# First stage of a two-layer attention and SSD kernel: order of the loads, tile-by-tile modulation, TensorE's order written out

## The chip, the cores and the metric

The kernel runs on one core of a Trainium2 chip. The metric is the device time of one execution in microseconds, the median of several runs. Inside a core, TensorE multiplies matrices, VectorE (DVE) and ScalarE (ACT) work on tensors elementwise, GpSimd (POOL) takes elementwise work as well, and SyncE's queue (SP) issues the loads and stores.

## What is computed

Two layers of a diffusion backbone run over 128 context tokens and 512 latent tokens, so five tiles of 128 tokens (tile 0 is the context), with width 1024. The change lies in the entry of layer 0: the normed input is scaled and shifted by a modulation that is itself a product of the condition with a weight, and is then projected to q, k, v and a gate.

```python
def rms_norm(x, w):
    y = xf * lax.rsqrt(jnp.mean(xf * xf, axis=-1, keepdims=True) + EPS)
    return y * w

def ada_mod(cond, mod_w, mod_b):
    m = jax.nn.silu(cond) @ mod_w + mod_b
    return jnp.split(m, 3, axis=-1)          # shift, scale, gate

def modulate(x, norm_w, shift, scale):
    return rms_norm(x, norm_w) * (1.0 + scale) + shift

def attn_qkvg(h, w_in, q_norm, k_norm):
    proj = h @ w_in
    q, k, v, g = jnp.split(proj, [...], axis=-1)
    ...
```

Behind it come attention with 16 heads over 4 key and value heads, the gated output projection, and layer 1 (a Mamba-2 mixer), which the change leaves alone.

## The kernel before

All products of activations and weights are made as three products of split operands: a value is cast to a high part (ScalarE, line 73), and the rest is a subtraction (VectorE or GpSimd, line 74); the pieces multiplied are high by high, high by low and low by high. The result keeps float32 accuracy.

The program is written as one stream of instructions. A planner with a timing model orders each engine's instructions and each queue's loads by itself, in the order of the text where nothing else speaks; each engine then executes its own list in that order and waits where an operand or a buffer isn't ready.

Layer 0 begins in `layer0` (line 285). The loads are issued in this order: the five tiles of x (line 328, 512 KB each; the small vectors `v0` of line 330 go in after the second), then four times a quarter: `load_mod(q)` (line 309) with four tiles of the modulation weight (512 KB each) and `load_kv(q)` (line 317) with 256 of the 1024 rows of the k, v weight (512 KB) and their split, whose subtractions run on GpSimd. A raw weight tile has two buffers.

Then the work, with the names of the program:

- `turned(t)` (line 339) takes a tile of x: sum of squares on ScalarE, reciprocal root on GpSimd (`norm_x`, line 226), scaling on VectorE, eight transposes on TensorE into `acc` and `pt`, and two copies back, one by ScalarE and one by VectorE.
- `mod(q)` (line 347) makes a quarter of shift and scale: 16 products into `pm` (each shows as two matmul instructions), a copy into `modrow` on ScalarE, four small products that turn the row into columns (line 357), and three small VectorE operations.
- `modded(q)` (line 366) applies them to two of the eight 128-row slices: for each slice once on tile 0 (128 columns) and once on tiles 1 to 4 together (512 columns), a scaling on VectorE into `hm`, the high part on ScalarE and the low part on VectorE, into `big`.
- `mm_kv(i, t, q)` (line 374) is the k (i = 0) or v (i = 1) product of a tile for a quarter: six matmuls into `acc`. There are 240 in all.

The text has all five `turned`, the columns of `v0`, then `mod(0)`, `modded(0)`, and for each quarter the next quarter's `mod` and `modded` ahead of the sixty matmuls of this one; in the third quarter the small vectors of layer 1 are prepared (`vectors`, line 152). At the end a ScalarE copy takes each tile's k and v to `kv` (line 396). Then `load_w` (line 255) loads and splits the first q weights, with subtractions on VectorE. `attention` (line 404) follows: it loads the first gate weights, norms and rotates k and q and starts the scores (line 630). Its q projection (line 283) writes into `S`, which takes the room of `acc`.

## Time and profile before

| | us |
|---|---|
| median of three runs | 1020.06 |
| lowest, highest | 1019.86, 1020.76 |
| span of the profiled execution, first to last instruction | 1016.4 |
| TensorE busy | 939.4 (92% of the span) |
| VectorE, ScalarE, GpSimd busy | 727.0, 549.4, 503.2 |
| mean granted TensorE clock | 0.978 |

The profiler gives the span of the execution that it recorded; that execution's time as the runs measure it is not listed. A timeline row has the start, the duration, the engine, the line of the program, the operation, what is written and read, and, in brackets, how long the engine had been idle before and what released it. Several equal instructions in a row are merged into one row (x4). PE is TensorE, SPq the issuing of SyncE's queue. [...]

### The profile page before, as it was taken

To read this page: it belongs to the slowest core of one execution; us is meant where nothing else is said; L and a number is where in the kernel's file an instruction comes from. 1 tells how busy PE (TensorE), PEld (TensorE's weight loads), DVE (VectorE), ACT (ScalarE), POOL (GpSimd) and SP (SyncE) were. 2 spreads that over 40 slices of the span, in tenths; PEclk is the share of its full clock that TensorE was granted. 3 is DMA by queue.
4 is the path that set the end of the run, shared out by engine and by line. 5 is a ranking of instruction groups with operands and counts; after the bars stand their busy time and mean duration, and the time that the engine had idled before them with its cause. 6 is when DMAs were issued, how large, how long until landed. Compare 5 with 4: busy or idle time off the path is not lost. (4 is left out here: it accounts for less than half of the span.)

```text
span 1016.4 us, 17297 instructions
## 1 busy us (share of the span) xinstructions
PE 939.4 (92%) x6522; PEld 847.7 (83%) x6522; DVE 727.0 (72%) x1094; ACT 549.4 (54%) x1272; POOL 503.2 (50%) x451
## 2 busy tenths in 40 slices
PE   5998999999999899989998898898988999889998
PEld 3898878989997789978997797788987999667786
DVE  5478665766776766757688788977688767996663
ACT  5346766757766653323465575567445664654340
POOL 3355325225450433445177679869487867642000
PEclk9999999999999999999999899998999999899999
DMA  9933242211122322333342345235324532446752
GB/s 312 350 120 104 92 142 89 84 52 43 42 64 84 104 87 102 125 100 96 99 137 91 104 147 171 68 129 160 111 90 133 178 110 89 135 147 193 256 194 100
DMA packets 90354, 127.91 MB, mean 126 GB/s; under 512 B 6816, under 2 KB 65312, under 8 KB 90272
## 3 DMA queue, kind: packets, MB, share of 16 engines
q1 hardware_dynamic: 90272, 126.82, 39.0%
q8 instruction: 51, 0.84, 0.3%
q14 instruction: 31, 0.25, 0.1%
HBM read 115.10 MB, written 11.70 MB: 125 GB/s over the span
## 5 line engine op out<-in xcount | busy, mean ns | idle before, releaser
L914 PE MATMUL pj<-h,wh 128*128 128x322 f32 (+1 forms) x1248 | 293.5, 320 | 6.2 <-DVE B L999 4.2
L74 POOL TENSOR_TENSOR wl<-raw,wh 128x512 fp32r<-128x512 f32 (+1 forms) x70 | 135.6, 1949 | 183.5 <-ACT wh L73 183.3
L914 PEld LDWEIGHTS pj<-h,wh 128*128 128x128 f32 (+1 forms) x1248 | 214.9, 192 | 11.0 <-issue 4.4
L914 PE MATMUL pj<-h,wl 128*128 128x322 f32 (+1 forms) x624 | 198.0, 318 | 0.0
L73 ACT CAST wh<-raw 128x1024 fp32r<-128x1024 f32 (+1 forms) x117 | 103.3, 912 | 81.8 <-DMA raw<-in_l_w_out 26.0
L914 PEld LDWEIGHTS pj<-h,wl 128*128 128x128 f32 (+1 forms) x624 | 120.2, 193 | 1.2 <-issue 0.2
L1140 ACT ACTIVATE am<-am,nb 128x128 f32<-128x128 f32 x320 | 98.6, 392 | 28.4 <-POOL am L1135 14.2
L283 PE MATMUL pp<-wh,big 128*128 128x256 f32 x576 | 113.4, 287 | 0.5 <-ACT sg L527 0.5
L283 PEld LDWEIGHTS pp<-wh,big 128*128 128x128 f32 x576 | 92.4, 191 | 0.7 <-ACT sg L527 0.7
L74 DVE TENSOR_TENSOR wl<-raw,wh 128x1024 fp32r<-128x1024 f32 x47 | 68.9, 1470 | 26.7 <-ACT wh L73 26.6
L283 PE MATMUL pp<-wl,big 128*128 128x256 f32 x288 | 81.8, 284 | 0.0
L74 DVE TENSOR_TENSOR pl<-pt,ph 128x512 fp32r<-128x512 f32 (+1 forms) x100 | 59.2, 600 | 25.9 <-ACT ph L73 25.0
L633 DVE TENSOR_REDUCE nm<-S 128x1 f32<-128x640 f32 x64 | 52.4, 820 | 13.6 <-PE S L630 12.7
L73 ACT CAST ph<-pt 128x512 fp32r<-128x512 f32 (+1 forms) x100 | 51.3, 518 | 18.8 <-PE pt L658 14.1
L637 ACT ACTIVATE Pt<-S,nm 128x640 f32<-128x640 f32 x64 | 51.3, 803 | 12.1 <-PE pt L658 9.5
L1141 POOL TENSOR_TENSOR am<-am,am 128x1024 f32<-128x1024 f32 x20 | 50.2, 2512 | 14.6 <-ACT am L1140 14.0
L1208 POOL TENSOR_TENSOR ys<-ys,ym 128x512 f32<-128x512 f32 x32 | 48.8, 1533 | 13.6 <-DVE ym L1207 13.6
L283 PEld LDWEIGHTS pp<-wl,big 128*128 128x128 f32 x288 | 55.0, 191 | 0.0
L658 PE MATMUL pt<-cst,Pt 128*128 128x128 f32 x320 | 50.8, 276 | 2.7 <-DVE pl L74 2.3
L630 PE MATMUL S<-kT,qT 128*128 128x320 f32 x256 | 50.6, 322 | 1.4 <-ACT Pt L637 1.4
L841 PE MATMUL a<-wh,big 128*128 128x256 f32 x256 | 46.8, 283 | 0.0
L658 PEld LDWEIGHTS pt<-cst,Pt 128*128 128x128 f32 x320 | 36.6, 141 | 11.9 <-PE S L630 3.8
(375 smaller groups left out, 2319.8 us busy)
## 6 DMA issues: line engine op xcount, KB each, us to landing
raw<-in_l_w_in SPq DMA_DIRECT2D x48, 512.0 KB
am<-acd SPq DMA_DIRECT2D x40, 512.0 KB
raw<-in_l_w_out SPq DMA_DIRECT2D x36, 512.0 KB
og<-in_l_mod_w SPq DMA_DIRECT2D x29, 512.0 KB
raw<-in_l_w_in SPq DMA_DIRECT2D x25, 256.0 KB
mw<-in_l_mod_w SPq DMA_DIRECT2D x11, 512.0 KB
raw<-in_l_mod_w SPq DMA_DIRECT2D x8, 512.0 KB
yzd<-ys SPq DMA_DIRECT2D x6, 640.0 KB
```

Source lines behind the costliest of these rows:

```text
L73: (heng.tensor_copy if heng else self.nc.scalar.copy)(hi, src)
L74: (eng or self.nc.vector).tensor_tensor(lo, src, r32(hi), op=ALU.subtract)
L283: nc.tensor.matmul(ps, a[:, k, cs], b[:, k, :], start=k == 0 and a is hi and b is w[0], stop=k == KD - 1 and a is lo)
L630: nc.tensor.matmul(S[:, 192 + 320 * q:512 + 320 * q], qTs[g, t][:, h, :], kT[:, hl, 320 * q:320 * q + 320], start=hl == 0, stop=hl == 1)
L633: nc.vector.tensor_reduce(c["m"], c["s"], axis=AX.X, op=ALU.max, negate=True)
L637: nc.scalar.activation(Pt, c["s"], AF.Exp, bias=c["m"], scale=1.0, accum_out=rss[g][t][:, h:h + 1])
L658: nc.tensor.transpose(pt[:, 2 * i + j, :], Pts[j][:, kt * P:kt * P + P], self.ident)
L841: self.nc.tensor.matmul(ps, self.ohl[a][:, k, ts], w[b][:, k, :], start=k == 0 and i == 0, stop=k == KD - 1 and i == 2)
L914: nc.tensor.matmul(ps[0:m, 190 + 322 * half:512 + 322 * half], w[b][:, k, off:off + m], hT[s][:, k, 322 * half:322 * half + 322], start=fi ...
L1140: nc.scalar.activation(af[d][:, h, :], af[d][:, h, :], AF.Exp, bias=self.nb[:, t, i:i + 1], scale=1.0)
L1141: nc.gpsimd.tensor_tensor(af[0], af[0], af[1], op=ALU.add)
L1208: nc.gpsimd.tensor_tensor(y, y, m, op=ALU.add)
```

## The change

The loads are issued in another order: the small vectors first, then tile 0 of x, the first quarter's modulation and k, v weights, then tiles 1 to 4 of x, then the other quarters. The split of a quarter's k, v weights is taken out of `load_kv` into `split_kv`, which stands behind the copy of that quarter's modulation row on ScalarE. `modded` takes a list of parts, so that the first quarter is modulated one tile at a time, with the next tile's `turned` ahead of this tile's matmuls. The second quarter's `mod` and `modded` follow after the first quarter's matmuls, and the third's and fourth's stand after two tiles of the quarter before. TensorE's instructions keep the written order from the columns to the last k, v matmul (`manual_schedule`). The vectors of layer 1 and the split of the first q weights are queued behind the last VectorE and ScalarE instructions of the stage (`issue_after`, an order on the engine's own list).

```diff
+    def last_on(self, engine):
+        return next(i for i in reversed(self.nc.cur_bb.bb.instructions) if i.engine == engine)
...
             def load_kv(q):
                 ks = slice(2 * q, 2 * q + 2)
-                raw = self.tl(self.wp, [P, 2, 512], tag="raw")
+                raw = raws[q] = self.tl(self.wp, [P, 2, 512], tag="raw")
                 nc.sync.dma_start(out=raw, in_=src[:, ks, D:D + 512])
-                for i, w in enumerate(wkv):
-                    self.split(w[0][:, ks, :], w[1][:, ks, :], raw[:, :, 256 * i:256 * i + 256], self.weng[0])
+
+            def split_kv(q):
+                ks = slice(2 * q, 2 * q + 2)
+                with tc.issue_after(self.last_on(mybir.EngineType.Activation)):
+                    for i, w in enumerate(wkv):
+                        self.split(w[0][:, ks, :], w[1][:, ks, :], raws[q][:, :, 256 * i:256 * i + 256], nc.gpsimd)
...
-            for t in range(NT):
-                nc.sync.dma_start(out=xs[:, t, :], in_=self.x_in(t))
-                if t == 1:
-                    v0 = self.column_rows(rp, "v0", 0, (("l0_norm_w", 8), ("l0_mod_b", 24)))
+            v0 = self.column_rows(rp, "v0", 0, (("l0_norm_w", 8), ("l0_mod_b", 24)))
             self.weng = [nc.gpsimd]
             for q in range(4):
+                if q == 0:
+                    nc.sync.dma_start(out=xs[:, 0, :], in_=self.x_in(0))
                 load_mod(q)
                 load_kv(q)
+                if q == 0:
+                    for t in range(1, NT):
+                        nc.sync.dma_start(out=xs[:, t, :], in_=self.x_in(t))
...
                 nc.scalar.copy(row, pm)
+                split_kv(q)
...
-            def modded(q):
+            def modded(q, parts=((0, 0, 1), (1, 1, NT - 1))):
                 for k in (2 * q, 2 * q + 1):
-                    for c, at, n in ((0, 0, 1), (1, 1, NT - 1)):
+                    for c, at, n in parts:
...
-            for t in range(NT):
-                turned(t)
-            self.columns(v0, 0, self.tl(pp, [P, 192], tag="pt"))
-            mod(0)
-            modded(0)
-            for q in range(4):
-                if q == 2:
-                    self.vectors(*vec, pp)
-                if q < 3:
-                    mod(q + 1)
-                    modded(q + 1)
+            with tc.manual_schedule(engines={mybir.EngineType.PE}):
+                self.columns(v0, 0, self.tl(pp, [P, 192], tag="pt"))
+                turned(0)
+                mod(0)
                 for t in range(NT):
+                    modded(0, ((min(t, 1), t, 1),))
+                    if t + 1 < NT:
+                        turned(t + 1)
                     for i in range(2):
-                        mm_kv(i, t, q)
-                    if q == 3:
-                        nc.scalar.copy(self.kv[:, :, 5 if t == 0 else t, :], acc[t].rearrange("p (a n) -> p a n", a=2))
-            w_q = self.load_w(self.wp, A["l0_w_in"], [(0, 256)])
+                        mm_kv(i, t, 0)
+                mod(1)
+                modded(1)
+                for q in range(1, 4):
+                    for t in range(NT):
+                        if q < 3 and t == 2:
+                            mod(q + 1)
+                            modded(q + 1)
+                        for i in range(2):
+                            mm_kv(i, t, q)
+                        if q == 3:
+                            nc.scalar.copy(self.kv[:, :, 5 if t == 0 else t, :], acc[t].rearrange("p (a n) -> p a n", a=2))
+            with ExitStack() as late:
+                for e in (mybir.EngineType.DVE, mybir.EngineType.Activation):
+                    late.enter_context(tc.issue_after(self.last_on(e)))
+                self.vectors(*vec, pp)
+                w_q = self.load_w(self.wp, A["l0_w_in"], [(0, 256)])
```

## Rows read from the trace of the kernel before

**Rows 1.** Windows over the first stage: TensorE at reduced clock, then without a gap.

```profile
22.99:27.10 4.11, 4.03 (x20) 2.79 (x21) 2.47 (x7) 1.44 (x3) 0.00 (x0) 0.58 1.08 360
27.10:62.68 35.58, 35.58 (x335) 32.22 (x334) 18.11 (x42) 16.48 (x32) 10.61 (x10) 1.00 0.88 290
```

**Rows 2.** Timeline, first modulation to first k, v matmul on TensorE; a weight's cast.

```profile
17.46 1.15 PE L352 MATMUL pm<-mw,sT 128*32 128x256 f32 x16
19.31 1.05 PE L357 MATMUL pt<-cst,modrow 128*128 128x2 f32 x8 [0.70 <-ACT modrow L354]
20.93 0.64 PE L352 MATMUL pm<-mw,sT 128*32 128x256 f32 x8 [0.57 <-DMA mw<-in_l_mod_w]
22.99 0.39 PE L379 MATMUL acc<-wh,big 128*128 128x256 f32 x1 [1.41 <-ACT big L73]
...
27.49 0.62 ACT L73 CAST wh<-raw 128x512 fp32r<-128x512 f32 x1 [2.74 <-DMA raw<-in_l_w_in]
```

**Rows 3.** Timeline of ScalarE, VectorE and TensorE around the end of the stage.

```profile
37.84 0.41 ACT L155 CAST selr<-pre 128x256 fp32r<-128x256 f32 x1
...
54.46 1.99 ACT L73 CAST wh<-raw 128x1024 fp32r<-128x1024 f32 x2
...
62.05 2.05 ACT L73 CAST wh<-raw 128x1024 fp32r<-128x1024 f32 x2
64.00 0.58 ACT L396 COPY kv<-acc 128x512 f32<-128x512 f32 x1
...
55.54 2.36 DVE L74 TENSOR_TENSOR wl<-raw,wh 128x1024 fp32r<-128x1024 f32 x2 [0.24 <-ACT wh L73]
...
64.64 0.58 PE L283 MATMUL S<-wh,big 128*128 128x256 f32 x1 [1.96 <-ACT kv L396]
```

**Rows 4.** A window behind the stage, and TensorE's last gap before the first scores.

```profile
62.40:88.00 25.60, 20.97 (x168) 20.57 (x166) 21.25 (x51) 11.45 (x31) 16.94 (x26) 0.93 0.21 63
...
87.56 0.54 PE L522 MATMUL pt<-identr,qs 128*128 128x128 f32 x4 [2.67 <-ACT qT L523]
```

**Rows 5.** Timeline of SyncE's queue: the small vectors among the tiles of x.

```profile
2.78 0.33 SPq L133 DMA_DIRECT2D v<-in_l_norm_w  x1
...
3.52 1.29 SPq L328 DMA_DIRECT2D x<-in_x_sample  x3
```

**Rows 6.** Timeline of tile 0, from its first read to its transposes.

```profile
5.52 0.63 ACT L232 ACTIVATE hm<-x 128x512 f32<-128x512 f32 x1 [1.79 <-DMA x<-in_x_prompt]
...
6.93 0.20 POOL L233 TENSOR_TENSOR ss<-sp 128x1 f32<-128x1 f32 x1 [6.51 <-ACT hm L232]
...
8.88 1.11 PE L344 MATMUL acc<-cst,x 128*128 128x128 f32 x4 [5.37 <-DVE x L235]
```

**Rows 7.** Timeline of GpSimd: half of the first k, v weight's split.

```profile
20.02 1.27 POOL L74 TENSOR_TENSOR wl<-raw,wh 128x512 fp32r<-128x512 f32 x1 [4.85 <-ACT wh L73]
```

**Rows 8.** TensorE's pieces: a window of line 379 alone, then timeline rows.

```profile
50.60:62.80 12.20, 11.43 (x95) 11.08 (x93) 1.00 0.54 170
...
16.26 0.66 PE L344 MATMUL acc<-cst,x 128*128 128x128 f32 x4
16.75 0.60 PE L344 MATMUL pt<-cst,x 128*128 128x128 f32 x4
...
45.45 1.93 PE L352 MATMUL pm<-mw,sT 128*32 128x256 f32 x32
...
50.60 0.95 PE L357 MATMUL pt<-cst,modrow 128*128 128x2 f32 x8
```

**Rows 9.** Groups by form, 0 to 62.7 us: busy and mean of VectorE's pieces.

```profile
L235 DVE TENSOR_SCALAR x<-x,ss 128x1024 f32<-128x1024 f32 x5 | 3.8, 758 | 5.8 <-POOL ss L90 5.7
L370 DVE TENSOR_SCALAR hm<-x,scale,shift 128x128 f32<-128x128 f32 x8 | 3.6, 455 | 0.1
L345 DVE COPY x<-pt 128x512 f32<-128x512 f32 x5 | 3.4, 686 | 1.1 <-PE pt L344 0.8
L74 DVE TENSOR_TENSOR big<-hm,big 128x128 fp32r<-128x128 f32 x8 | 3.4, 423 | 0.0
```

More of the change, by code (lines that the diff above doesn't have):

```diff
@@ L306, in layer0 @@
             mods = A["l0_mod_w"].rearrange("(k p) n -> p k n", p=P)
-            mws, nmw = {}, [0]
+            mws, nmw, raws = {}, [0], {}
             def load_mod(q):
```

## The prediction

> **What bounds the kernel now.** I read the windows by stage first, then the timeline of TensorE over the first 70 us, then the waits of the other engines. TensorE is the bound almost everywhere. [...] The end of the stage is [rows 3]: the last k, v result is copied only at 64.00 us, because two casts of the gate weights stand ahead of it on ScalarE, and the q projection starts at 64.64 us. The q weights had been cast and split long before, at 54.46 and 55.54 us, beside TensorE's work. After that, [rows 4]: from 62.4 to 88 us VectorE is busy 21.25 of 25.6 us, and TensorE idles 2.67 us before the first scores. So whatever the change does to the first stage is worth what it does to the end of the k, v matmuls (62.68 us, the 64.64 less the 1.96 of wait), plus what it does to the handover behind it.
>
> **Arrivals.** The loads come one after the other. Tile 0 of x, the first of them, is read from 5.52 us on [rows 6]. The first tile of the second modulation is the 11th half-megabyte transfer and is awaited until 20.93; the second k, v weight is the 15th and is awaited until 27.49 [rows 2]: 15.41 / 10 = 1.54 and 21.97 / 14 = 1.57 us each. I take 1.55. After the change the two small vector loads stand ahead of x, 3.52 - 2.78 = 0.74 us [rows 5], so tile 0 is there at 6.26. Then come four modulation tiles (the last at 6.26 + 4 x 1.55 = 12.46, about 5 us earlier than now by the same count), the k, v weight (14.01), and only then tile 1 of x, as 7th: 15.56 us, where it now lands at about 7.1. The second modulation stays 11th to 14th: 26.41 us at its last, no earlier than now.
>
> [...]
>
> **Tile 0 and the first modulation.** From landing to transposes a tile takes 8.88 - 5.52 = 3.36 us [rows 6]. Tile 0 is transposed from 9.6 us and the 16 modulation products follow, to about 15.2 us at the clock that rises on the way. The row is copied (idle 0.70) and turned into columns (1.05), then VectorE, ScalarE and VectorE make the first input: first k, v matmul possible at 17.5 to 18.5 us, against 22.99. That is what the change gains, some 5 us.
>
> **But TensorE's order is fixed,** and it has the transposes of tile 1 ahead of the matmuls of tile 0. They cannot start before 15.56 + 3.36 = 18.92 us. More likely they wait for GpSimd: the k, v weight's casts are now tied behind the row's copy (15.9 us), its two subtractions take 1.27 us each [rows 7] and would end near 19.0, and tile 1's sum of squares, queued behind them, needs another 8.88 - 6.93 = 1.95 us [rows 6] to the transposes: 20.95. I take 20.0 us. Queued behind this wait are tile 0's twelve matmuls and all else on TensorE.
>
> **From there to the end of the stage,** TensorE's work at full clock [rows 8]: transposes of four tiles at 1.1 us (16.26 to 17.35), 4.4; 240 k, v matmuls at 11.43 / 95 = 0.12, 28.8; three modulations at 1.93, 5.8; three turns into columns at 0.95, 2.85. Together 41.9 us. To that come the waits of the written order:
> - each turn into columns stands directly behind its modulation, so it waits the 0.70 us for the row's copy [rows 2] three times: 2.1. Now only the first one waits; in the other three other matmuls stand between.
> - all of tile-by-tile work for the first quarter ends before the second modulation begins, and that one's input is then awaited with nothing behind it that could run: at present 22.99 - 20.36 = 2.6 us from the end of the columns to the matmul [rows 2], less where the scaling is quicker. I take 1.6, between 1.2 and 2.6.
> - the clock: TensorE has idled for some 3 to 4 us before tile 1's transposes, as it had before 22.99, and 4.11 us at 0.58 cost 1.7 us [rows 1]. And VectorE needs for a tile 0.76 + 0.69 + 2 x (0.46 + 0.42) = 3.2 us [rows 9] (the means hold a few instructions stretched beside GpSimd; about 2.6 without), since the first quarter is now scaled in ten pieces of 128 columns instead of two of 128 and two of 512; TensorE needs 1.1 + 12 x 0.12 = 2.5. Four tiles at that difference are 0.4 to 2.8 us. The two overlap, since a slow TensorE hides a slow VectorE. I take 2.0 for both.
>
> End of the k, v matmuls: 20.0 + 41.9 + 2.1 + 1.6 + 2.0 = 67.6 us, against 62.68: 4.9 us later. The least is 18.92 + 41.9 + 2.1 + 1.2 = 64.1 (1.4 later), and full overlap of what I counted twice could take 1 us from it; the most 20.95 + 41.9 + 2.1 + 2.6 + 1.7 + 2.8 = 72.0 (9.4 later). The second and third modulation wait for no transfer: they are reached after 40 us, when by the same count their tiles are there (the 24th transfer, 41.9, is the last that matters).
>
> **The handover.** The casts of the q weights are tied behind the last copy of k, v on ScalarE, so the cover that they had is gone. After the last matmul: 0.1 us (the 0.70 of [rows 2] less the row's copy, an estimate) and a copy of 0.58, a small cast of 0.41, the cast of the first half, 1.0, its subtraction on VectorE, 2.36 / 2 = 1.2 [rows 3]: the second matmul of the projection stands 3.3 us behind the end, where the projection starts 1.96 us behind it now, 1.3 later. The gate weights' casts, which delayed that copy, are no longer there, since their buffers come free only after the q weights' split. For VectorE the two subtractions (2.36) now fall into the stretch of [rows 4], where it is the busy one; those of the gate weights go further back. Bounds: -2.67 us (VectorE's chain to the first scores is relieved of the gate weights and TensorE's idle goes) and +2.4 (all of the subtractions on that chain). I take 1.3. The vectors of the second layer move behind the stage too; nobody needs them for hundreds of microseconds, and I cost them at nothing, up to 0.5 us of VectorE.
>
> **Sum:** 4.9 + 1.3 = 6.2 later. The profiled execution has a span of 1016.4 us, and its own time outside the profiler is not listed; the median of the three runs, 1020.06, lies 3.7 above the span, and I keep that. I take off 0.3 for overlap counted twice: span 1022.3, time 1026.0 us.
>
> **Rivals.**
> - *Break-even, no change.* Tile 1 is normalised before GpSimd takes the weights (18.92 us), the clock stays up, VectorE keeps pace: 1.4 later, and 0 to 1.3 at the handover less some of the 2.67: 1020.06 + 1.4 = 1021.5. For it speaks that GpSimd's queue is planned, not written; against, that three things must go well at once. 0.17.
> - *Faster.* The end of the stage is the least, 1.4 later less the 1 us of overlap, but with no gate weight casts ahead of it the last k, v copy comes at once and VectorE's chain to the first scores is free from 63 to 67 us: both idles behind the stage, 1.96 [rows 3] and 2.67 us [rows 4], go. 1020.06 + 0.4 - 4.6 = 1015.9; half of it 1018. It decides where the q weights' split takes less than those idles; by [rows 3] it takes 3.3. 0.15.
> - *The planner keeps x first.* Only TensorE's order is written out; the queue of loads is still planned. If the x tiles still come first, the first modulation ends near 19.3, tile 1's transposes follow its columns at 21.1, and the stage ends at 21.1 + 41.9 + 2.1 + 1.6 + 0.5 = 67.2: again 1020.06 + 4.5 + 1.3 = 1026. It changes the reason, not the time. 0.06.
> - *The main case,* slower: 0.62, own range 1022 to 1032.
>
> About 0.2% (2 us) is what a measurement of this kernel can tell from no change. Faster 0.15, same 0.17, slower 0.68. The range, 1017.5 to 1031.5, leaves out some 0.1 at each end: a handover that gives more than half of the faster rival, and the sum of the upper bounds.
>
> **What would show it.** In the profile after: the first k, v matmul at 20 to 22 us, not 18; an idle time on TensorE ahead of tile 1's transposes released by VectorE's scaling; the second modulation after 32 us, followed by idle time of 1 to 2.6 us released by ScalarE's cast; the last k, v matmul at 67 to 68 us; the q weights' casts behind the last k, v copy and the q projection 2 to 3.3 us after the last matmul. I am wrong if the last k, v matmul ends by 63 us, or if the first scores (87.94 now) do not come later though it does; and my sum says nothing of the 930 us behind, which are planned anew with every change and may move either way.

## The result, and the profile after

The kernel after takes 1042.34 us, median of four runs (1040.16 to 1042.47), against 1019.96 for the kernel before on the same chip: ratio 1.023, 95% interval 1.0207 to 1.0254. It is slower, as forecast, but by 22.4 us where 6 were forecast, and outside the range. The profiled executions have spans of 1040.7 and 1016.4 us. Of the 24.3 between them, 17.3 are there when the last k, v matmul starts (79.68 against 62.40), 2.0 more at the first scores (107.2 against 87.9), and 5.0 come in the 930 us behind, which are planned anew.

The page's line of busy times: TensorE is busy only 6.4 us longer than before, part of it at a lower granted clock (mean 0.968 against 0.978). The rest is waiting.

```profile
PE 945.8 (91%) x6522; PEld 854.0 (82%) x6522; DVE 730.3 (70%) x1106; ACT 550.1 (53%) x1278; POOL 505.4 (49%) x451
```

TensorE's timeline of the kernel after: start, duration, engine, line, operation, out<-in, and in brackets the idle time before and what ended it. These lines answer [rows 2] and [rows 6].

```profile
9.68 1.12 PE L353 MATMUL acc<-cst,x 128*128 128x128 f32 x4 [5.46 <-DVE x L238]
...
11.58 3.64 PE L361 MATMUL pm<-mw,sT 128*32 128x256 f32 x32
15.92 1.05 PE L367 MATMUL pt<-cst,modrow 128*128 128x2 f32 x8 [0.70 <-ACT modrow L363]
22.29 1.11 PE L353 MATMUL acc<-cst,x 128*128 128x128 f32 x4 [5.31 <-DVE x L238]
...
27.69 0.66 PE L353 MATMUL acc<-cst,x 128*128 128x128 f32 x4 [1.21 <-DVE x L238]
...
32.39 0.81 PE L353 MATMUL acc<-cst,x 128*128 128x128 f32 x4 [2.16 <-DVE x L238]
...
37.24 0.66 PE L353 MATMUL acc<-cst,x 128*128 128x128 f32 x4 [0.77 <-DVE x L238]
...
47.55 0.58 PE L389 MATMUL acc<-wh,big 128*128 128x256 f32 x1 [2.44 <-ACT big L76]
```

Up to 16.9 us everything stands where the prediction put it: tile 0 at 9.68 (forecast 9.6), the modulation to 15.2 (15.2), the row's 0.70. The clock, which the prediction has rising there, reads 1.00 from 9.68 to 15.22; what the rows show is the pace: the 32 products take 3.64 us, where 32 took 1.93 at 45.45 before [rows 8], and four transposes 1.12 us at 9.68, where four took 0.66 at 16.26 before. From 22.29 on, the transposes of tiles 1 to 4 stand 5.40, 4.70 and 4.85 us apart, and each of them waits for VectorE's scaling. The prediction had about 3.0 us for a tile (2.5 of TensorE and a quarter of the 2.0). This is the view that it lacked: not how much work a tile is, but how far apart the tiles come.

Windows of the kernel after, with the columns of [rows 1]: length, then busy time and instructions of PE, PEld, DVE, ACT, POOL, the granted TensorE clock as a share of full speed, the busy share of the DMA engines, GB/s. (The first window of [rows 8] has those of PE and PEld alone.)

```profile
16.97:22.29 5.32, 0.01 (x1) 0.00 (x1) 3.45 (x8) 1.74 (x6) 2.94 (x5) 0.70 1.07 362
22.29:27.00 4.71, 4.19 (x20) 3.98 (x20) 1.73 (x6) 2.22 (x7) 0.94 (x3) 0.61 1.08 359
27.69:41.30 13.61, 10.68 (x72) 10.10 (x72) 6.69 (x17) 5.82 (x17) 1.90 (x6) 0.87 1.04 324
47.55:53.60 6.05, 5.85 (x24) 5.25 (x24) 2.48 (x7) 1.44 (x3) 0.00 (x0) 0.53 0.31 89
```

No engine is full between 27.69 and 41.30: TensorE is busy 10.68 of 13.61 us, VectorE 6.69, ScalarE 5.82. What paces the tiles is a chain through all four engines. The timeline of ScalarE, GpSimd and VectorE shows it, first for tile 1 (16.81 to 19.54), then for tile 2:

```profile
16.81 0.63 ACT L235 ACTIVATE hm<-x 128x512 f32<-128x512 f32 x1
...
19.07 0.56 ACT L76 CAST big<-hm 128x128 fp32r<-128x128 f32 x2 [1.54 <-DVE hm L380]
19.54 0.62 ACT L235 ACTIVATE hm<-x 128x512 f32<-128x512 f32 x1
...
23.44 0.59 ACT L354 COPY x<-acc 128x512 f32<-128x512 f32 x1 [3.19 <-PE acc L353]
23.92 0.64 ACT L235 ACTIVATE hm<-x 128x512 f32<-128x512 f32 x1
...
24.55 0.49 ACT L76 CAST big<-hm 128x128 fp32r<-128x128 f32 x2
24.94 0.62 ACT L235 ACTIVATE hm<-x 128x512 f32<-128x512 f32 x1
...
25.73 0.19 POOL L236 TENSOR_TENSOR ss<-sp 128x1 f32<-128x1 f32 x1 [4.29 <-ACT hm L235]
...
19.40 0.55 DVE L77 TENSOR_TENSOR big<-hm,big 128x128 fp32r<-128x128 f32 x2
...
26.88 0.75 DVE L238 TENSOR_SCALAR x<-x,ss 128x1024 f32<-128x1024 f32 x1 [1.21 <-POOL ss L93]
```

ScalarE idles 3.19 us for tile 1's transposes, copies them, squares the first half of tile 2 (23.92), casts both modulated slices of tile 1 (24.55), and only then squares the second half of tile 2 (24.94). The sum on GpSimd, VectorE's scaling (26.88) and TensorE's transposes of tile 2 (27.69) follow one after the other. At tile 3 both squares (28.87, 29.63) come ahead of the casts (30.26), but still behind the copy of tile 2 (28.39); tile 4 is like it. By the rows nothing but ScalarE's list held tile 2's squares back during the 3.19 us: the last reader of tile 0's modulated slices, VectorE at 19.40, is done at 19.95, and with the same order of loads e13 below reads tile 2 of x from 17.90. The squares of a tile have become a link of the chain that ends with the transposes of that tile, and the next turn begins with the copy of those. Before the change all five tiles were squared (the last half from 12.97 us) ahead of any modulated slice (21.35).

### The profile page after: what moved, and what is told of

Its sections match the earlier page's. It is cut to its first block, busy times and chain, and to the rows that moved or that the text cites. A ratio compares the mean times of both kernels' runs of the same rounds, so it can differ in the third digit from the quotient of the medians.

```text
span 1040.7 us, 17302 instructions
## 1 busy us (share of the span) xinstructions
PE 945.8 (91%) x6522; PEld 854.0 (82%) x6522; DVE 730.3 (70%) x1106; ACT 550.1 (53%) x1278; POOL 505.4 (49%) x451
## 5 line engine op out<-in xcount | busy, mean ns | idle before, releaser
L76 ACT CAST wh<-raw 128x1024 fp32r<-128x1024 f32 (+1 forms) x117 | 103.2, 912 | 83.2 <-DMA raw<-in_l_w_out 22.4
L77 DVE TENSOR_TENSOR wl<-raw,wh 128x1024 fp32r<-128x1024 f32 x47 | 71.9, 1536 | 26.4 <-ACT wh L76 26.3
L76 ACT CAST ph<-pt 128x512 fp32r<-128x512 f32 (+1 forms) x100 | 51.5, 518 | 21.6 <-PE pt L677 16.9
```

The lines of the kernel that those rows point to most:

```text
L76: (heng.tensor_copy if heng else self.nc.scalar.copy)(hi, src)
L77: (eng or self.nc.vector).tensor_tensor(lo, src, r32(hi), op=ALU.subtract)
```

## Experiments

Times of the stage by run, from the timelines (start of tile 1's transposes, of the last k, v matmul, of the first scores, and from there to the end of the span), and the ratio of the run times to the kernel before on the same chip:

| kernel | tile 1 | last k, v | scores | behind | ratio [95%] |
|---|---|---|---|---|---|
| before | 10.81 | 62.40 | 87.9 | 928.5 | 1 |
| after | 22.29 | 79.68 | 107.2 | 933.5 | 1.023 [1.0207, 1.0254] |
| e15 after, again | 22.20 | 79.58 | 107.2 | 933.6 | 1.0237 [1.0199, 1.0274] |
| e1 squares to another buffer | 23.09 | 73.51 | 99.9 | 945.0 | 1.0193 [1.0161, 1.0225] |
| e13 squares a tile earlier | 19.53 | 73.83 | 102.6 | 929.7 | 1.015 [1.013, 1.017] |
| e2 old load order | 26.52 | 85.82 | 112.3 | 936.6 | 1.0298 [1.026, 1.0336] |
| e5 TensorE's order planned | 21.34 | 70.59 | 100.4 | 931.4 | 1.0184 [1.0141, 1.0226] |
| e7 second modulation earlier | 21.97 | 75.81 | 104.4 | 929.5 | 1.017 [1.013, 1.021] |
| e14 more work for TensorE | 22.00 | 78.76 | 107.6 | 930.0 | 1.0214 [1.0192, 1.0236] |
| e6 tiles turned together | 19.38 | 68.97 | 98.2 | 929.8 | 1.011 [1.0089, 1.0131] |
| e11 = e1 + e5 | 20.21 | 63.56 | 93.7 | 925.7 | 1.0086 [1.0055, 1.0118] |
| e3 no tie of the q weights | 21.76 | 81.94 | 106.9 | 927.9 | 1.0182 [1.0154, 1.021] |
| e10 = e1 + e3 + e7 | 22.58 | 71.57 | 95.6 | 934.0 | 1.0125 [1.0097, 1.0152] |
| e12 = e1 + e3 + e5 | 21.06 | 65.65 | 90.8 | 938.9 | 1.0108 [1.0085, 1.0131] |
| e4 before, new load order | 18.79 | 67.81 | 93.3 | 928.0 | 1.0062 [1.0043, 1.008] |
| e8 before, q weights tied | as before | 63.27 | 92.1 | 929.8 | 1.0058 [1.003, 1.0086] |
| e9 before, gate weights tied | as before | 61.85 | 87.3 | 928.6 | 1.0049 [1.0031, 1.0066] |

The stretch behind the scores scatters from 926 to 939 us whatever was edited in the first stage (945.0 in e1, whose profiled execution was also the slowest of its four, 1046.71 against 1035.17 to 1039.41). Which execution was profiled matters too: that of e11 was the fastest of its five (1021.24, median 1028.16), that of e9 the fastest of its twelve. And the ratios of e1, e3, e5, e7 and e14 have intervals that overlap with that of the kernel after; those of e6, e10, e11, e12 and e13 lie below it, that of e2 above. So causes are read from the stage columns, in which the two executions of the kernel after (the second is e15) agree within 0.1 us.

### The squares: e1, e13

`norm_x` writes its squares, which nobody reads, to a buffer of tag `hm` (three of them), and `modded` takes its slices from the same three. e1 gives the squares the tile's PSUM bank instead:

```diff
-    def norm_x(self, x, wp):
+    def norm_x(self, x, wp, out=None):
-            sq = self.tl(wp, [P, 512], tag="hm", bufs=3)
+            sq = self.tl(wp, [P, 512], tag="hm", bufs=3) if out is None else out
...
-                self.norm_x(xs[:, t, :], rp)
+                self.norm_x(xs[:, t, :], rp, acc[t])
```

> The squares of the input norm are written into the tile's own accumulator bank (acc[t], not yet in use) instead of one of the three shared hm buffers; all else as after the change. Theory A (three hm buffers, shared by the squares of tile t+1 and the modulated slices of tile t, put tile t+1's norm on ScalarE behind tile t's modulation; the transposes of tiles 1 to 4 then stand 4.8 to 5.4 us apart): the spacing falls to 2.5 to 3.2 us, the last first-quarter matmul moves from 41.2 to about 33 to 35 us, the last k, v matmul from 79.9 to 70 to 73 us, and the time by 6 to 9 us, to 1033 to 1036. Theory B (the tiles of x land too late): spacing and time stay within 1 us. Theory C (TensorE's written order alone, with its waits in series): spacing stays above 4 us, time within 2 us.

Measured: the last k, v matmul 6.2 us earlier. A window of e1 from tile 1's transposes to the second modulation, and ScalarE's timeline in it:

```profile
23.09:35.60 12.51, 12.51 (x93) 12.20 (x93) 8.87 (x23) 4.82 (x14) 2.76 (x6) 0.88 1.09 352
```

```profile
22.63 0.58 ACT L235 ACTIVATE acc<-x 128x512 f32<-128x512 f32 x1
...
24.22 0.59 ACT L354 COPY x<-acc 128x512 f32<-128x512 f32 x1 [0.88 <-PE acc L353]
```

The last square of the last tile is done at 23.2 us, ahead of tile 1's copy; TensorE is busy 12.51 of 12.51 us and the tiles stand 3.78, 2.31 and 2.30 us apart. But this edit changes two things: the buffers, and with them the order in which ScalarE gets its work. e13 keeps the three buffers and only issues each tile's norm one tile further ahead:

```diff
-                self.norm_x(xs[:, t, :], rp)
...
+                self.norm_x(xs[:, 0, :], rp)
                 turned(0)
+                self.norm_x(xs[:, 1, :], rp)
                 mod(0)
                 for t in range(NT):
+                    if t + 2 < NT:
+                        self.norm_x(xs[:, t + 2, :], rp)
```

> The changed kernel, with each tile's norm (squares, sum, reciprocal root) issued in the text one tile further ahead: tile 1's before the first modulation, tile t+2's before tile t is modulated. Buffers, loads and TensorE's written order of transposes, turns and matmuls are unchanged. Theory A (what spaces the tiles is ScalarE's order of work, with the next tile's squares behind this tile's casts; a buffer more would only have freed that order): the tiles' transposes stand 2.5 to 3.2 us apart instead of 4.7 to 5.4, the last k, v matmul starts at 72 to 74 us instead of 79.7, and the ratio to the kernel before is 1.015 to 1.02. Theory B (three shared buffers set the pace whatever the order): spacing stays at 4.5 us or more and the last k, v matmul stays within 1.5 us of 79.7, ratio 1.02 to 1.025.

TensorE's and ScalarE's timeline of e13:

```profile
19.53 1.10 PE L352 MATMUL acc<-cst,x 128*128 128x128 f32 x4 [1.46 <-DVE x L238]
...
24.77 1.05 PE L352 MATMUL acc<-cst,x 128*128 128x128 f32 x4
...
27.88 0.60 PE L352 MATMUL acc<-cst,x 128*128 128x128 f32 x4
...
31.34 0.60 PE L352 MATMUL acc<-cst,x 128*128 128x128 f32 x4
...
17.90 0.63 ACT L235 ACTIVATE hm<-x 128x512 f32<-128x512 f32 x1
...
24.09 0.63 ACT L235 ACTIVATE hm<-x 128x512 f32<-128x512 f32 x1
...
25.86 0.59 ACT L353 COPY x<-acc 128x512 f32<-128x512 f32 x1 [0.85 <-PE acc L352]
```

The last square (24.09) now stands ahead of tile 2's copy, transposes of tiles 2 to 4 follow TensorE's own work (no bracket), and the last k, v matmul comes 5.75 us earlier than in e15. TensorE's idle time between tile 1's transposes and the second modulation falls from 4.1 us (1.21, 2.16 and 0.77 after the change) to 0.9 (0.29 and 0.56). The tiles do not come as evenly as theory A had it, but 5.24, 3.11 and 3.46 us apart; the 5.24 hold 4.95 us of TensorE's own work, in which a half tile's transposes take 1.10 and 1.06 us and most matmuls 0.41, where those from 27.88 take 0.60 and 0.28.

The gain is nearly as large as e1's, but it is made up in another way. In e13 2.7 us of it are there at tile 1 (19.53 against 22.20 in e15), and from there to the second modulation it takes 15.94 us, where e1 takes 12.51 and the kernel after 19.12. In e1 tile 1 comes 0.8 us later than after the change, although its squares are done by 18.1 us: GpSimd's list there has the sum of tile 2, which waits 0.96 us for ScalarE (20.77), ahead of the reciprocal root of tile 1.

With the same three buffers all but 0.9 us of the idle time is gone. So the cost is ScalarE's order of work; the shared buffers were how the planner came to that order, as the other order in e1 shows, not what held the tiles apart. The rows after the change show that order at work: ScalarE idles 3.19 us ahead of tile 1's copy (23.44), with the squares of tile 2 (23.92) behind it on the list.

### The late tiles of x: e2, e4

e2 is the changed kernel with the loads in the old order; e4 is the kernel before with the loads in the new one.

```diff
-            v0 = self.column_rows(rp, "v0", 0, (("l0_norm_w", 8), ("l0_mod_b", 24)))
+            for t in range(NT):
+                nc.sync.dma_start(out=xs[:, t, :], in_=self.x_in(t))
+                if t == 1:
+                    v0 = self.column_rows(rp, "v0", 0, (("l0_norm_w", 8), ("l0_mod_b", 24)))
             for q in range(4):
-                if q == 0:
-                    nc.sync.dma_start(out=xs[:, 0, :], in_=self.x_in(0))
                 load_mod(q)
                 load_kv(q)
-                if q == 0:
-                    for t in range(1, NT):
-                        nc.sync.dma_start(out=xs[:, t, :], in_=self.x_in(t))
```

> After the change, but with the loads in the order of the kernel before (x tiles first, small vectors after the second); the rest stays. Theory A: the first modulation ends at about 19 instead of 15.2 us and the transposes keep their spacing of about 5 us; the last k, v matmul is 1 to 4 us later than 79.9 and the time 1042 to 1046. Theory B (late x tiles): the transposes stand under 3 us apart and the last k, v matmul comes 5 to 10 us earlier, time 1032 to 1037. Theory C: first modulation later, so 3 to 4 us slower.

> The kernel before with the new order of the loads alone; TensorE's order is the planner's, the modulation in one piece, the splits and the q weights as before. By the prediction's count of arrivals the first modulation is ready 5 us sooner and the x tiles 8 us later; the planner can run the modulation meanwhile. Theory A (shared hm buffers and written order are what costs, not the arrivals): the last k, v matmul within 3 us of 62.7 us and the time within 3 us of before. Theory B (late x tiles cost): last k, v matmul 4 us later or more, time 4 us or more above before.

(e4's edit is the same diff read backwards, on the kernel before.) TensorE's timeline of e2, the transposes of tiles 1 to 4:

```profile
26.52 1.12 PE L351 MATMUL acc<-cst,x 128*128 128x128 f32 x4 [4.88 <-DVE x L238]
...
31.92 1.12 PE L351 MATMUL acc<-cst,x 128*128 128x128 f32 x4 [0.86 <-DVE x L238]
...
37.07 0.66 PE L351 MATMUL acc<-cst,x 128*128 128x128 f32 x4 [0.92 <-DVE x L238]
...
42.01 0.73 PE L351 MATMUL acc<-cst,x 128*128 128x128 f32 x4 [2.40 <-DVE x L238]
```

All of x is loaded ahead of the modulation weights here, and the tiles still stand 5.40, 5.15 and 4.94 us apart. The late tiles of x are refuted as the cause of the spacing. Within the changed kernel the new load order gains: the stage ends 6.1 us later without it, where 1 to 4 were expected. In the program of before the same order loses 5.4 us. By its size that is theory B of e4, and there the late tiles do cost: TensorE idles 5.67 us ahead of tile 1's transposes, and the planner keeps the transposes of tiles 1 to 4 ahead of the turn into columns. TensorE in e4:

```profile
18.79 1.11 PE L346 MATMUL acc<-cst,x 128*128 128x128 f32 x4 [5.67 <-DVE x L235]
...
30.95 0.58 PE L381 MATMUL acc<-wh,big 128*128 128x256 f32 x1
```

The first k, v matmul stands at 30.95 us, 8.0 later than before, although the first modulation's products were done by 13.1 instead of 18.6 us. The load order is worth nothing by itself; its sign is decided by the order of the work behind it.

### TensorE's written order: e5, e7, e6

e5 leaves TensorE's order to the planner:

```diff
-            with tc.manual_schedule(engines={mybir.EngineType.PE}):
+            with ExitStack():
```

> After the change, but TensorE's order in the stage is left to the planner (no manual_schedule). Theory C (the written order is what costs): the planner fills the waits with the second modulation and other tiles' matmuls, the last k, v matmul comes at 64 to 69 us and the time at 1024 to 1030. Theory A (shared hm buffers): the first quarter still ends after 38 us, but the waits are filled in part; last k, v matmul at 72 to 78 us, time 1035 to 1041.

Measured: tile 0's matmuls now go ahead of tile 1's transposes (first k, v matmul 18.48 instead of 23.91), the second modulation's products fill gaps between the tiles, and the stage ends 9.1 us earlier, although the tiles stay 5.5 to 6.0 us apart. The 70.59 lies between the ranges of theory C and theory A: the written order is one cost, and the spacing of the tiles remains as another. e7 keeps the written order and moves one step of it, the second modulation, ahead of the last tile's matmuls:

```diff
                 for t in range(NT):
                     modded(0, ((min(t, 1), t, 1),))
                     if t + 1 < NT:
                         turned(t + 1)
+                    if t == NT - 1:
+                        mod(1)
+                        modded(1)
                     for i in range(2):
                         mm_kv(i, t, 0)
-                mod(1)
-                modded(1)
```

> After the change, but the second modulation and its input stand ahead of the fifth tile's first-quarter matmuls instead of behind them. By the prediction's term for the exposed chain (1.6 us, bounds 1.2 and 2.6; the trace after shows 2.44 us of idle time and a clock of 0.80 from 47.5 to 62 us): the idle time before the second quarter shrinks by about 1.4 us, and if the low clock behind it comes from that gap, the second quarter gains up to 3 us more: last k, v matmul 1.4 to 5 us sooner than 79.9. If the gap's place doesn't matter: within 1 us.

Its timeline of TensorE and a window from the second modulation to the third:

```profile
45.36 0.39 PE L389 MATMUL acc<-wh,big 128*128 128x256 f32 x1 [0.93 <-ACT big L76]
...
49.76 1.93 PE L361 MATMUL pm<-og,sT 128*32 128x256 f32 x32
```

```profile
39.20:50.00 10.80, 8.59 (x82) 6.56 (x85) 5.38 (x13) 3.59 (x8) 2.51 (x2) 1.00 0.51 148
```

3.9 us earlier, of which two parts make 3.2: the idle time for the modulated input is 0.93 instead of 2.44 us, and the 24 matmuls behind it take 49.76 - 45.36 = 4.4 us at a granted clock of 1.00, where they took 6.05 at 0.53. Another 0.5 is there at tile 4's transposes, ahead of the edit (36.76 against 37.24).

e6 writes another order: all tiles turned first, the first quarter modulated in two pieces, the first two modulations ahead of the first k, v matmul.

```diff
-                for t in range(NT):
-                    modded(0, ((min(t, 1), t, 1),))
-                    if t + 1 < NT:
-                        turned(t + 1)
-                    for i in range(2):
-                        mm_kv(i, t, 0)
+                for t in range(1, NT):
+                    turned(t)
+                modded(0)
                 mod(1)
                 modded(1)
-                for q in range(1, 4):
+                for q in range(4):
                     for t in range(NT):
-                        if q < 3 and t == 2:
+                        if 0 < q < 3 and t == 2:
```

> After the change, but all five tiles are normalised and transposed before the first quarter is modulated, that in pieces of 128 and 512 columns as before, and the first two modulations stand ahead of the first k, v matmul; loads, written order and ties as after. Theory A: no tile waits in the shared buffers for another's modulation, so the fifth tile's transposes stand at 24 to 26 us, the first k, v matmul at 27 to 29 us, then no idle time on TensorE; last k, v matmul at 63 to 66 us, scores 17 to 14 us sooner than after (107.2), time 2 to 7 us above before. Theory C (the written order costs whatever it holds): last k, v matmul after 70 us.

The first k, v matmul stands at 31.25 us, 7.3 later than after the change, and the last one at 68.97, 10.7 earlier; both are later than expected (27 to 29, 63 to 66). An early start of TensorE's main work is worth nothing if its pieces then come apart.

### TensorE's clock: e14, e15

e14 gives TensorE transposes of the identity, unused, where it idles:

```diff
+            def keep_busy(n):
+                d = self.tl(pp, [P, 512], tag="pm", bufs=1)
+                for i in range(n):
+                    nc.tensor.transpose(d[:, 0:P], self.ident, self.ident)
...
                 mod(0)
+                keep_busy(28)
...
                 mod(1)
+                keep_busy(14)
                 modded(1)
```

> The changed kernel with additional transposes of the identity on TensorE, whose results nobody uses: 28 behind the first modulation's turn into columns and 14 behind the second's, where TensorE idles for 5.3 and 2.4 us. Theory (some of the lost time is TensorE's clock, granted at 0.61 in the 4.7 us behind the first idle time and 0.53 in the 6.05 us behind the second): granted clock above 0.9 in both stretches, the matmuls behind the second modulation take 3.2 us instead of 6.05, and the last k, v matmul starts 2.5 to 4.5 us earlier, at 75 to 77. Rival (the clock there hides behind VectorE's and ScalarE's work, so nothing is won): last k, v matmul within 1 us of 79.7, or later by what the added transposes themselves take.

e15 is the changed kernel unchanged, beside it.

> The changed kernel as it is, on the same chip and in the same rounds as the two others, to have their differences from it directly: ratio to the kernel before 1.02 to 1.025, last k, v matmul within 0.5 us of 79.7.

The last k, v matmul comes 0.8 us earlier: the rival. Windows of e14:

```profile
26.70:31.39 4.69, 3.34 (x20) 3.05 (x20) 2.45 (x6) 2.32 (x7) 0.95 (x3) 0.65 1.08 346
...
46.86:52.68 5.82, 5.25 (x25) 4.50 (x25) 2.48 (x7) 1.44 (x3) 0.00 (x0) 0.71 0.30 90
```

and of e15, also from one tile's transposes to the next:

```profile
27.59:32.29 4.70, 2.54 (x20) 2.34 (x20) 2.45 (x6) 2.32 (x7) 0.95 (x3) 1.00 1.10 350
```

The same step from tile 2 to tile 3 takes 4.69 us at a granted clock of 0.65 and 4.70 at 1.00: here the clock hides behind the chain through ScalarE. The step before it, from tile 1 to tile 2, takes 5.39 us at 0.65 in e15 and 4.70 at 1.00 in e14, 0.7 us less. Of these 0.46 lie between the start of tile 1's transposes and ScalarE's copy of them (1.15 against 0.69 us); the rest goes with ScalarE's order, which in e14 has both squares of tile 2 ahead of the casts. Behind the second modulation the added transposes did not do what they were for: TensorE was busy 4.58 of the 6.15 us before 46.86 at clock 1.00, idled 0.86 and 0.48 us for its inputs, and the clock fell to 0.71. What the clock costs there is read from e7 instead: 6.05 - 4.4 = 1.65 us.

### The handover: e3, e8, e9

e3 takes the tie of the vectors and q weights out of the changed kernel, e8 puts that of the q weights into the kernel before:

```diff
-            with ExitStack() as late:
-                for e in (mybir.EngineType.DVE, mybir.EngineType.Activation):
-                    late.enter_context(tc.issue_after(self.last_on(e)))
-                self.vectors(*vec, pp)
-                w_q = self.load_w(self.wp, A["l0_w_in"], [(0, 256)])
+            self.vectors(*vec, pp)
+            w_q = self.load_w(self.wp, A["l0_w_in"], [(0, 256)])
```

> After the change, but the vectors of layer 1 and the split of the first q weights aren't tied behind the stage's last VectorE and ScalarE instructions. By the handover term of the prediction (1.3 us, bounds -2.7 and 2.4): the q projection starts 1 to 2 us behind the last k, v matmul with all of its weights there, the first scores come 1 to 2 us sooner relative to it, and the time falls by 1 to 2 us. Rival: the tie costs nothing, because VectorE's chain of k sets the first scores anyway: within 0.7 us. Second rival: without the tie the casts push into the stage's ScalarE work and the last k, v matmul comes later: slower by 1 us or more.

> The kernel before with one thing added: the split of the first q weights is tied behind the last VectorE and ScalarE instructions of the stage. By the handover term of the prediction: the last k, v matmul unchanged, the second matmul of the q projection 1.3 us later than now, first scores 0 to 2.4 us later, time 0 to 2.5 us above before. Rival: the q weights' load now holds the buffers longer, the gate weights come later and VectorE's chain to the scores lengthens: 3 to 5 us.

The end of the stage in the kernel after, ScalarE, VectorE and TensorE, which answers [rows 3]:

```profile
79.99 0.59 ACT L411 COPY kv<-acc 128x512 f32<-128x512 f32 x1 [0.83 <-PE acc L389]
...
80.78 1.99 ACT L76 CAST wh<-raw 128x1024 fp32r<-128x1024 f32 x2
...
83.17 0.20 DVE L438 TENSOR_SCALAR qw<-qw 128x64 f32<-128x64 f32 x1 [2.31 <-DMA qw<-in_l_q_norm]
...
83.62 1.75 DVE L77 TENSOR_TENSOR wl<-raw,wh 128x1024 fp32r<-128x1024 f32 x1
...
81.88 0.50 PE L286 MATMUL S<-wh,big 128*128 128x256 f32 x2 [1.93 <-ACT wh L76]
85.42 0.58 PE L286 MATMUL S<-wl,big 128*128 128x256 f32 x1 [2.93 <-DVE wl L77]
```

The cast comes right behind the last copy, as forecast. The subtraction does not: VectorE's list has the small scaling of the q norm ahead of it, that one waits 2.31 us for a transfer, and TensorE idles 2.93 us a second time. e8 shows the same wait, added to the kernel before:

```profile
66.72 0.20 DVE L425 TENSOR_SCALAR qw<-qw 128x64 f32<-128x64 f32 x1 [2.55 <-DMA qw<-in_l_q_norm]
...
68.96 0.58 PE L286 MATMUL S<-wl,big 128*128 128x256 f32 x1 [3.17 <-DVE wl L77]
```

From the last k, v matmul to the first scores the tie costs 92.1 - 63.27 = 28.8 against 25.5 before, 3.3 us in e8. That is the size of the rival, not of the term; the rows show the wait for the q norm in the place of the cause that the rival named. In e3 that stretch is 25.0, 2.5 shorter than after, but the stage itself ends 2.3 later; the q projection waits for the last copy alone (1.90 us, at 84.12), so the first cast of the q weights is back ahead of that copy. At the first scores the tie costs 0.3 us there. By the ratios e3's time is about 5 us shorter than after, more than its scores; the rest lies behind them, within the scatter, and stays open.

e9 ties the first gate weights in the kernel before, to take away the two casts that delay its last copy in [rows 3]:

```diff
+                        self.last_kv = self.last_on(mybir.EngineType.Activation)
...
-        w_g = self.load_w(self.wp, A["l0_w_in"], [(GG, 256)])
+        with tc.issue_after(self.last_kv):
+            w_g = self.load_w(self.wp, A["l0_w_in"], [(GG, 256)])
```

> The kernel before, with the casts of the first gate weights tied behind the last copy of k, v on ScalarE. In the kernel before, that copy stands behind two of these casts (2.05 us) and the q projection starts 1.96 us behind the last k, v matmul. If the copy is what the projection waits for: it starts 0.6 to 0.9 us behind, the first scores and the time come 1 to 1.4 us sooner. Rival: VectorE's chain of k sets the first scores, or the gate weights become late: within 0.5 us, or slower by up to 2 us.

```profile
62.80 0.39 PE L286 MATMUL S<-wh,big 128*128 128x256 f32 x1 [0.68 <-ACT kv L399]
```

TensorE's idle time at this line of e9 is 0.68 instead of 1.96 us and the scores come 0.6 earlier, where 1 to 1.4 were expected; the time is still 0.5% longer. The profiled execution was the fastest of twelve (1017.73 us, median 1023.10), and its span of 1015.9 us is 0.5 shorter than before the change: no row shows where the other executions lose, and the cause stays open.

### The parts together: e10, e11, e12

e11 has the edits of e1 and e5, e12 those and e3's, e10 those of e1, e3 and e7. The edits of e11:

```diff
-                self.norm_x(xs[:, t, :], rp)
+                self.norm_x(xs[:, t, :], rp, acc[t])
...
-            with tc.manual_schedule(engines={mybir.EngineType.PE}):
+            with ExitStack():
```

> After the change with three of its costs taken out together, loads and TensorE's written order kept: squares in the accumulator bank, second modulation ahead of the fifth tile's first-quarter matmuls, q weights not tied. If the three costs add (6.3 us, 3.9 us at the last k, v matmul, 2 to 2.5 us at the handover, each from its run alone): last k, v matmul at 69 to 71 us, first scores at 94 to 96, time 6 to 10 us above before. If the first two remove the same idle time: last k, v matmul at 72 to 74 us, time 9 to 13 us above before.

> After the change with the squares in the accumulator bank and TensorE's order left to the planner. Alone the first brought the last k, v matmul 6.3 us forward, the second 9.2. If the written order costs only because the normalisation of the tiles crawls (theory A), the two overlap: last k, v matmul at 67 to 71 us, time 9 to 15 us above before. If they are separate costs (theory C beside A): 63 to 66 us, time 4 to 8 us above before.

> As the run with squares in the accumulator bank and the planner's order on TensorE, and the q weights not tied in addition. The tie cost 3.6 us at the first scores when added to the kernel before, and 2.4 when taken out of the changed one: first scores 2 to 4 us nearer to the last k, v matmul than in that run, time 2 to 6 us lower. If the untied casts get in the way of the stage, the last k, v matmul comes 1 to 3 us later and half of that is lost.

TensorE in e11:

```profile
17.32 0.58 PE L389 MATMUL acc<-wh,big 128*128 128x256 f32 x1 [2.44 <-ACT big L76]
...
20.21 1.05 PE L353 MATMUL acc<-cst,x 128*128 128x128 f32 x4
...
21.91 0.70 PE L353 MATMUL acc<-cst,x 128*128 128x128 f32 x4
...
23.55 0.66 PE L353 MATMUL acc<-cst,x 128*128 128x128 f32 x4
```

The last k, v matmul of e11 stands at 63.56: 16.1 of the 17.3 us are back with two edits (6.2 and 9.1 alone, 15.3 together by addition), and the first k, v matmul stands at 17.32, the 17.5 that the prediction had for a tile 0 that nothing holds back. e10 gives 8.1 where its parts make 6.2 + 3.9 - 2.3 = 7.8. The two costs add up and account for the stage. None of these kernels is faster than the one before. In e11 1.2 us are left at the last k, v matmul and 5.8 at the first scores: the handover, with its two idle times of 1.92 and 3.18 us, costs 4.6 more than before. e12, without the tie, has that stretch at 25.1 us instead of 30.1, but its last k, v matmul comes 2.1 later; its scores are 2.9 us earlier than e11's, and its time, expected 2 to 6 us lower, is not lower (1.0108 against 1.0086).

## Why the prediction was wrong

The direction and the places were right; the step that failed is "From there to the end of the stage". Term by term, for the end of the k, v matmuls:

| term | forecast | measured | difference |
|---|---|---|---|
| tile 1's transposes | 20.0 | 22.29 | +2.3 |
| to the second modulation (transposes, 60 matmuls, clock and cadence) | 13.6 | 41.41 - 22.29 = 19.1 | +5.5 |
| second modulation, row copy, columns | 3.6 | 3.7 | +0.1 |
| its exposed chain | 1.6 | 2.44 | +0.8 |
| 180 matmuls, two modulations | 28.8 | 79.95 - 47.55 = 32.4 | +3.6 |
| end | 67.6 | 79.95 | +12.3 |

- **Tile 1 at 20.0.** Arrival (15.56 forecast; in e13, where nothing stands ahead of it, ScalarE reads the tile at 15.16) and GpSimd's split (its end 19.0, as forecast) were right. The wait has another cause: ScalarE's list has the casts of tile 0 between the two squares of tile 1 (16.81 and 19.54), and those casts wait 1.54 us for VectorE. With the squares ahead, in e13, tile 1 stands at 19.53, within the bounds (18.92 to 20.95).
- **Clock and VectorE's cadence, 2.0.** This is the term that was mis-sized. I priced a tile by the busiest single engine (3.2 us of VectorE against 2.5 of TensorE) and let the tiles overlap. In the planned order they don't: copy, squares (at tile 2 with the casts between them), sum, scaling, transposes is one chain of 4.7 to 5.4 us. The rows for each link were there, [rows 6] above all, whose 3.36 us from a tile's square to its transposes I used for the arrival of tile 1 alone and not for tiles 2 to 4. Shown by e1 and e13: 6.2 and 5.75 us at the end of the stage. In e1, with the squares out of the chain, the stretch that was forecast at 13.6 and took 19.1 takes 12.51.
- **The exposed chain, 1.6.** Inside its bounds (1.2 to 2.6) at 2.44, and the lower clock came with it (0.53 behind it, against 1.00 behind the 0.93 us of e7): 1.65 us more by e7, at a place where the sum had none. The clock ahead of that, which the sum did have, cost half a microsecond at one tile and nothing at the next (e14).
- **180 matmuls and two modulations, 28.8.** Nearly all of the 3.6 us more is in the first 24 of these matmuls: 6.05 us where the sum had 2.9. The clock is 1.65 of it; the other 1.5 are there at a clock of 1.00 too, in e7, where the 24 take 4.4 us and TensorE waits another 0.49 for VectorE's part of the modulated input. The sum priced the wait up to the first of these matmuls alone.
- **The written order.** The prediction saw that tile 0's matmuls and all else queue behind tile 1's transposes, but costed it only once, as a later start. e5 shows it again at every tile: with slow tiles, TensorE's fixed order gives away 9.1 us, because tile 0's matmuls may not go ahead of tile 1's transposes and the second modulation may not fill the gaps; how much each is worth is not shown.
- **The handover, +1.3.** Measured 2.0, inside the bounds and of the right sign. The chain named (copy, cast, subtraction) was right and lacked one wait: the second matmul stands 5.5 us behind the end of the last one, not 3.3, since VectorE's list has an instruction with a late transfer ahead of the subtraction (e3, e8), and the subtraction took 1.75 us, not 1.2.
- **The rivals.** Of the faster one's two idle times the 2.67 ahead of the scores shrank to 0.58, but the 1.96 stayed as 1.93 and a new one of 2.93 came. The planner did not keep x first. The range failed because its upper bound, 72.0, added the largest price of each named piece, and the chain through ScalarE was not among them.
- **Behind the stage.** 5.0 us of the difference of the spans lie there; the scatter of other kernels is as large, and no cause is shown.

## What to carry to other kernels

When work is cut from one batch into a pipeline of pieces, price a piece by the longest chain through all engines for one piece, in the order in which each engine gets its instructions, and only then by the busiest engine. A written order for one engine turned such waits into idle time here (9.1 us, by e5), so write out what should fill it, or leave the order free. And look at what stands ahead on an engine's list when work is moved to a new place: a small instruction with a late transfer is enough (2.31 us of wait here).

## What was not expected of the hardware

- The clock granted to TensorE fell behind short idle times although it had been busy: in e14 from 1.00 over 6.15 us with 4.58 busy to 0.71 in the 5.82 us behind, with idle times of 0.86 and 0.48 us. In e7, with 8.59 of 10.80 us busy and idle times of 0.93 and 0.49, it stayed at 1.00.
- VectorE's scaling of a whole tile, 0.75 us at 26.88 in the kernel after, took 1.75 in e13 while GpSimd split a weight: 1.0 us more, beside a subtraction of 1.27 that had begun 0.07 us earlier. The kernel before has the like, as the prediction noted of its means: three scalings of 128 columns took 1.96 us at 21.35, beside GpSimd's split (to 22.52), and 1.06 at 34.70, with GpSimd idle. No run shows why. VectorE and GpSimd in e13:

```profile
17.72 1.75 DVE L238 TENSOR_SCALAR x<-x,ss 128x1024 f32<-128x1024 f32 x1 [5.15 <-POOL ss L93]
...
17.65 1.27 POOL L77 TENSOR_TENSOR wl<-raw,wh 128x512 fp32r<-128x512 f32 x1
```

- The loads ran at 359 to 362 GB/s (windows 16.97 to 27.00 of the kernel after), 1.45 us for a half megabyte; 1.55 was forecast.
